# Cumulative log decays of a gated DeltaNet block: one transpose, a trip through DRAM and row broadcasts in place of products with ones

## The chip, the cores and the metric

The kernel runs on one core of one Trainium2 chip, in one launch. The metric is the device time in microseconds (us) of that core, the median of several runs. Below, PE is TensorE (matmuls), PEld its weight loads, DVE is VectorE, ACT is ScalarE, POOL is GpSimd, SP is SyncE, whose queue issues most of the loads.

## What is computed

One layer of a hybrid encoder over 1024 tokens of width 1024, in float32: an RMSNorm, one input projection, a gated DeltaNet group (4 heads of 128) and a latent attention group (8 heads) side by side, an output projection, then a squared-ReLU MLP. The part that matters here is the decay of the DeltaNet group. The reference works in chunks of 64 tokens; the kernel does the same mathematics in blocks of 128.

```python
beta = sigmoid(b_logit)
log_a = -exp(a_log) * softplus(a_logit + dt_bias)      # (tokens, heads)
g = cumsum(log_a, axis=-1)                             # inside each chunk
gdiff = g[..., :, None] - g[..., None, :]
decay_strict = exp(where(strict, gdiff, -inf))
decay_causal = exp(where(causal, gdiff, -inf))
a_mat = einsum("bhnid,bhnjd->bhnij", k_beta, k) * decay_strict
t_inv = triangular_solve(eye + a_mat, eye)
p = einsum("bhnid,bhnjd->bhnij", q, k) * decay_causal
q_dec = q * exp(g)[..., None]
```

So for every head two things are wanted from the cumulative sums g: a 128x128 matrix of exp(g_i - g_j) for each of 8 blocks, and the row exp(g) repeated on all partitions, to scale the transposed queries.

## The kernel before, in words

**Stages.** Up to 74 us the input is normalised and transposed and the narrow columns of the projection are made. From about 74 to 297 us lies the stage that the change touches: PE projects q, k and v (`project`, L582 on, the matmuls at L207 to L209, three for each product), with the latent queries and keys beside them, and the DeltaNet heads get ready. From 297 to 345 us the scan over the blocks runs, then attention, the output projection and the MLP follow.

**Who sets the order.** The tasks of the second stage are Python generators, and a small planner (`Weave`, L44) runs them: each `yield step(pe, dve, act, pool, lat)` adds planned costs to the planner's clock, `signal(name, delay)` sets the planned time of an event, and `yield "name"` or `need(tag, n)` waits for an event or for n free tiles of the pools "a" (12 tiles) and "b" (9 tiles of 128x1024 f32). The order in which they come out is the program's order; the framework's scheduler then places the instructions in the queues of the engines, each of which works its queue off in order. A wait at the head of a queue holds up what stands behind it.

**The weights.** Each 512 KB weight tile is loaded by SP (L183, buffers of 3), rounded by ACT to a high part `whi` (L198), and DVE makes the low part `wlo` (L199). The products of a projection need both.

**Decays.** `decays` (L410 on) makes the log decays `loga` [128 tokens, head, block] and, with two small products (L441, L442) into one PSUM bank `ps_gc`, their cumulative sums in columns, `gcol`, as well as `eg`, `egl` and `cdec`. Its event "decays" lets the first head start.

**head_k(h)** (L641 on) needs the same sums as rows on all partitions. POOL fills `rg` with the triangle `upper` times the head's log decays (L647), PE multiplies that with a matrix of ones (L659, two calls of 512 columns), so that each partition of `ps_g` holds the row of cumulative sums. ACT takes the exponential of one partition (L660, `erow`), and eight DVE instructions (L663) subtract `gcol` and apply the mask `neg` to give E; ACT sends the row to DRAM (L667, `d_er`) and takes the exponential of E (L668). Later in `head_k` the keys are transposed (L620, L622), their squares are summed (L682), small operations of a reciprocal square root follow (L155 to L167), and A is products of keys times E (L698, L702), sent to DRAM (L705, `d_A`).

**head_q(h)** reads the keys (L714) and the row exp(g), repeated on all partitions (L715, `er` from `d_er`), multiplies PT by E (L725) and the queries by `er` on POOL (L731), and sends PT and that product out (L726, L732).

**What follows.** `substitute` reads pieces of all four A (L759, `N`) and solves the 32x32 blocks on DVE in 31 steps (L769, L775). `levels` combines them with products on PE (L817), and the scan starts when all levels are done.

Of the kernel before, what the change touches and what calls it, by code (L numbers as in the profile page):

```python
# [11 lines left out]
AF = mybir.ActivationFunctionType  # L12
# [5 lines left out]
P = 128  # L18
# [78 lines left out]
def need(tag, n):  # L97
    return "need", tag, n


def step(pe=0.0, dve=0.0, act=0.0, pool=0.0, lat=0.4):
    return pe, dve, act, pool, lat


def build(tc, a, out):
# [24 lines left out]
    def psum(name, tag="ps"):  # L130
        return pp[0].tile([P, HALF], F32, name=name, tag=tag, bufs=pp[1][tag])
# [83 lines left out]
    def scratch(name, *shape):  # L215
        return dp.tile(list(shape), F32, name=name)
# [4 lines left out]
    d_v = scratch("d_v", P, NT, MH, 64)  # L221
    d_q = scratch("d_q", MH * 64, T)
    d_r = scratch("d_r", MH * ROPE, T)
    d_er = [scratch(f"d_er{h}", T) for h in range(GH)]
    d_kT = scratch("d_kT", GH, P, T)
    d_qd = scratch("d_qd", GH, P, T)
    d_PT = scratch("d_PT", GH, P, T)
# [27 lines left out]
    def btile(name, dt=F32):  # L255
        W.live["b"] += 1
        return lbp.tile([P, T], dt, name=name, tag="b", bufs=NB)

    def free(tag, n=1):
        W.live[tag] -= n  # L260

    def half_tile(name):
        return lp.tile([P, HALF], F32, name=name, tag="hf", bufs=3)
# [16 lines left out]
    def blocks3(t):  # L280
        return t.rearrange("p (b i) -> p b i", i=P)
# [128 lines left out]
    def decays():  # L410
        spt = btile("spt")
        xx, ax, ee, zz, z2, sp = (spt[:, i * 32 : (i + 1) * 32].rearrange("p (h t) -> p h t", h=GH) for i in range(6))
        nc.vector.tensor_tensor(xx, aL, cols[:, C_DT : C_DT + GH].unsqueeze(2).to_broadcast(shp), op=ALU.add)
        nc.vector.scalar_tensor_tensor(ax, xx, -1.0, xx, op0=ALU.mult, op1=ALU.max)
        e1 = nc.scalar.activation(ee, ax, AF.Exp, scale=-1.0).ins
        e2 = nc.scalar.activation(ealog, cols[:, C_ALOG : C_ALOG + GH], AF.Exp).ins
        after(e2, e1, "tables in turn")
        nc.scalar.activation(beta, bL, AF.Exp, scale=-1.0)

        nc.vector.tensor_scalar(zz, ee, 2.0, None, op0=ALU.add)  # L420
        nc.vector.reciprocal(zz, zz)
        nc.vector.tensor_mul(zz, zz, ee)
        nc.vector.tensor_mul(z2, zz, zz)
        nc.vector.tensor_scalar(sp, z2, 1.0 / 19.0, 1.0 / 17.0, op0=ALU.mult, op1=ALU.add)
        for n in (15, 13, 11, 9, 7, 5, 3, 1):
            nc.vector.tensor_mul(sp, sp, z2)
            nc.vector.tensor_scalar(sp, sp, 1.0 / n, None, op0=ALU.add)
        nc.vector.scalar_tensor_tensor(sp, sp, 2.0, zz, op0=ALU.mult, op1=ALU.mult)
        nc.vector.scalar_tensor_tensor(sp, xx, 0.0, sp, op0=ALU.max, op1=ALU.add)
        nc.vector.scalar_tensor_tensor(  # L430
            loga, sp, -1.0, ealog.unsqueeze(2).to_broadcast(shp), op0=ALU.mult, op1=ALU.mult
        )
        nc.vector.tensor_scalar(beta, beta, 1.0, None, op0=ALU.add)
        nc.vector.reciprocal(beta, beta)
        free("b")
        W.signal("decays", 7.0)
        yield step(0.0, 4.0, 2.0, lat=7.0)

        ps = psum("ps_gc")
        la = loga.rearrange("p h t -> p (h t)")  # L440
        mm(ps[:, 0:32], upper, la, start=True, stop=True)  # L441
        mm(ps[:, 32:64], ones, la, start=True, stop=True)  # L442
        g, gl = (ps[:, i : i + 32].rearrange("p (h t) -> p h t", h=GH) for i in (0, 32))
        nc.vector.tensor_copy(gcol, g)
        nc.scalar.activation(egl, gl, AF.Exp)
        nc.vector.tensor_sub(cdec, gl, gcol)
        nc.scalar.activation(eg, gcol, AF.Exp)
        nc.scalar.activation(cdec, cdec, AF.Exp)
        nc.vector.tensor_scalar(eg, eg, -1.0, None, op0=ALU.mult)
        yield step(0.2, 0.5, 0.8)  # L450


    NF = ROPE // 2
# [187 lines left out]
    def head_k(h):  # L641

        yield f"k{h - 1}" if h else "decays"
        yield need("a", 2)
        yield need("b", 2)
        rg = btile(f"rg{h}")
        nc.gpsimd.tensor_tensor(  # L647
            blocks3(rg),
            upper.unsqueeze(1).to_broadcast([P, NT, P]),
            loga[:, h, :].unsqueeze(2).to_broadcast([P, NT, P]),  # L650
            op=ALU.mult,
        )
        Es[h] = E = atile(f"E{h}")
        erow = btile(f"erow{h}")
        yield step(pool=2.3)
        for half in range(2):
            s = slice(half * HALF, (half + 1) * HALF)
            ps = psum("ps_g")
            mm(ps, ones, rg[:, s], start=True, stop=True)  # L659
            nc.scalar.activation(erow[0:1, s], ps[0:1, :], AF.Exp)  # L660
            for b in range(4):
                bb = 4 * half + b
                nc.vector.scalar_tensor_tensor(  # L663
                    E[:, bb * P : (bb + 1) * P], ps[:, b * P : (b + 1) * P], gcol[:, h, bb : bb + 1], neg,
                    op0=ALU.subtract, op1=ALU.min,
                )
        nc.scalar.dma_start(d_er[h].unsqueeze(0), erow[0:1, :])  # L667
        nc.scalar.activation(E, E, AF.Exp)  # L668
        free("b", 2)
        yield step(1.7, 2.1, 2.2)  # L670

        yield f"k{h}"
        _, kT = ys.pop(("k", h))
        nc.scalar.dma_start(d_kT[h], kT)
        ktok[h] = atile(f"ktok{h}")
        token_major(kT, ktok[h])
        kj = lp.tile([P, P], F32, name=f"kj{h}", tag="kj")
        for b in range(NT):  # L680
            s = slice(b * P, (b + 1) * P)
            nc.vector.scalar_tensor_tensor(  # L682
                kj, ktok[h][:, s], 1.0, ktok[h][:, s], op0=ALU.mult, op1=ALU.mult, accum_out=ssk[:, h, b : b + 1]
            )
        nc.vector.tensor_scalar(ssk[:, h, :], ssk[:, h, :], EPS, None, op0=ALU.add)
        nc.vector.reciprocal(ck[:, h, :], ssk[:, h, :])
        nc.vector.tensor_mul(ck[:, h, :], ck[:, h, :], beta[:, h, :])
        nc.vector.tensor_mul(cdec[:, h, :], cdec[:, h, :], ck[:, h, :])
        r = rsqrt(ssk[:, h, :], [NT], "nkr")
        nc.vector.tensor_mul(nk[:, h, :], r, ssk[:, h, :])  # L690
        yield step(0.9, 2.8, 1.2)
        yield need("b", 1)
        A = btile(f"A{h}")
        for b4 in range(2):
            ps = psum("ps_kk")
            for j in range(4):
                s = slice((4 * b4 + j) * P, (4 * b4 + j + 1) * P)
                mm(ps[:, j * P : (j + 1) * P], kT[:, s], kT[:, s], start=True, stop=True)  # L698
            for j in range(4):
                b = 4 * b4 + j  # L700
                s = slice(b * P, (b + 1) * P)
                nc.vector.scalar_tensor_tensor(  # L702
                    A[:, s], ps[:, j * P : (j + 1) * P], ck[:, h, b : b + 1], E[:, s], op0=ALU.mult, op1=ALU.mult
                )
        nc.scalar.dma_start(d_A[h], A)  # L705
        free("b", 2)
        W.signal(f"A{h}", 3.0)
        yield step(1.7, 2.1)

    def head_q(h):  # L710
        yield f"q{h - 1}" if h else "k3"
        yield need("b", 3)
        kT, er, PT = (btile(f"{n}{h}") for n in ("kTq", "er", "PT"))
        nc.sync.dma_start(kT, d_kT[h])  # L714
        nc.sync.dma_start(er, d_er[h].partition_broadcast(P))  # L715
        yield f"q{h}"
        sq, qT = ys.pop(("q", h))
        nc.scalar.activation(sq, qT, AF.Square)
        for b4 in range(2):
            ps = psum("ps_kq")  # L720
            hs = slice(4 * b4 * P, 4 * (b4 + 1) * P)
            for j in range(4):
                s = slice((4 * b4 + j) * P, (4 * b4 + j + 1) * P)
                mm(ps[:, j * P : (j + 1) * P], kT[:, s], qT[:, s], start=True, stop=True)
            nc.vector.tensor_tensor(PT[:, hs], ps, Es[h][:, hs], op=ALU.mult)  # L725
        nc.sync.dma_start(d_PT[h], PT)  # L726
        psq = psum("ps_q2")
        for b in range(NT):
            mm(psq[:, b : b + 1], sq[:, b * P : (b + 1) * P], ones[:, 0:1], start=True, stop=True)
        nc.vector.tensor_scalar(tq[:, h, :], psq[:, 0:NT], EPS, DK * EPS, op0=ALU.add, op1=ALU.mult)  # L730
        nc.gpsimd.tensor_tensor(er, er, qT, op=ALU.mult)  # L731
        nc.sync.dma_start(d_qd[h], er)  # L732
        Es.pop(h)
        free("b", 5)
        free("a")
        W.signal(f"q done {h}")
        yield step(1.8, 1.3, 1.1, 2.3)
# [989 lines left out]
```

## Time and profile before

| | |
|---|---|
| median of 3 runs | 1267.82 us (1267.79 to 1269.14) |
| the profiled execution, its own time | 1267.6 us |
| its span in the trace | 1265.9 us |
| PE busy | 1220.9 us, 96% of the span, 6228 instructions |
| DVE busy | 898.9 us, 71% |
| ACT busy | 655.2 us, 52% |
| POOL busy | 160.1 us, 13% |
| mean granted TensorE clock | 0.992 |

The span is what the trace covers; 1.7 us of the execution's own time lie outside it. Matmuls overlap in the array, so their durations add up to more than the time they take, and a busy PE is not PE at its peak. All times in the trace are counted from the span's start.

### The profile page before, as it was taken

What the parts mean: (1) busy time and instruction counts of PE and PEld (TensorE: products, weight loads), DVE (VectorE), ACT (ScalarE), POOL (GpSimd) and SP (SyncE); (2) the same over time, 40 slices, a digit from 0 to 9 for tenths busy, and PEclk for the clock granted to TensorE, in tenths of its full rate; (3) what the DMA queues carried; (4) which work ended last, traced back from release to release, by engine and by line L of the source; (5) the groups of instructions that cost most, each with busy time, mean ns of one, the idle gap of its engine ahead of it and who ended that gap; (6) DMA issues with size and microseconds to landing.
All of it is one profiled execution on the core that took longest, in us unless ns stands there. A gap on an engine that the chain in (4) does not pass through costs nothing.

```text
span 1265.9 us, 17687 instructions
## 1 busy us (share of the span) xinstructions
PE 1220.9 (96%) x6228; PEld 1032.8 (82%) x6228; DVE 898.9 (71%) x1779; ACT 655.2 (52%) x1201; POOL 160.1 (13%) x148
## 2 busy tenths in 40 slices
PE   7999999999899999999899999999999999999997
PEld 6978888899778878887677888888888888888885
DVE  7678879545646776695986777767666787875665
ACT  6467744326645786675646444445445433343441
POOL 1011001220044553421000000000000000010120
PEclk9999999999999999999989999999999999999999
DMA  5124634735352511123445455554449984656821
GB/s 235 33 77 147 191 121 167 239 80 172 102 154 83 168 50 30 42 68 133 167 162 162 162 179 208 175 191 184 161 161 401 406 308 154 196 175 220 294 75 66
DMA packets 111218, 205.72 MB, mean 163 GB/s; under 512 B 33557, under 2 KB 51989, under 8 KB 111130
## 3 DMA queue, kind: packets, MB, share of 16 engines
q1 hardware_dynamic: 93696, 171.90, 40.6%
q10 hardware_dynamic: 17434, 32.70, 7.0%
q8 instruction: 49, 0.80, 0.3%
q14 instruction: 39, 0.32, 0.1%
HBM read 143.07 MB, written 61.49 MB: 162 GB/s over the span
## 4 chain that ended last, share of the span: by engine, by line
PE 61%; ACT 4%; DVE 4%; DMA 2%; issue 1%; POOL 0%; ACTq 0%; SPq 0%; DVEq 0%; POOLq 0%
PE ps_dn L208 8%; PE ps_dn L209 8%; PE ps_dn L207 8%; PE ps_up L207 7%; PE ps_up L208 7%; PE ps_up L209 7%; PE ps_PT L1061 2%; PE ps_out L207 2%; PE ps_out L209 2%; PE ps_out L208 2%; PE ps_o L1080 1%; PE ps_sc L207 1%; PE ps_o L1079 1%; PE ps_sc L208 1%; PE ps_sc L209 1%
## 5 line engine op out<-in xcount | busy, mean ns | idle before, releaser
L1589 POOL TENSOR_TENSOR rows<-rows,gpost 128x512 f32<-128x512 f32 x12 | 20.1, 1708 | 612.0 <-ACT junk L1586 612.0
L209 PE MATMUL ps_proj<-hThi,wlo 128*128 128x512 f32 x192 | 75.1, 395 | 1.2 <-DVE wlo L199 1.2
L207 PE MATMUL ps_proj<-hThi,whi 128*128 128x512 f32 x192 | 76.1, 396 | 0.0
L208 PE MATMUL ps_proj<-hTlo,whi 128*128 128x512 f32 x192 | 76.1, 396 | 0.0
L1065 DVE TENSOR_TENSOR PTlo<-ps_PT,PThi 128x512 fp32r<-128x512 f32 (+2 forms) x96 | 52.0, 549 | 20.0 <-ACT PThi L1064 19.3
L1064 ACT CAST PThi<-ps_PT 128x512 fp32r<-128x512 f32 (+2 forms) x96 | 45.4, 480 | 30.0 <-PE ps_PT L1061 28.5
L1521 DVE TENSOR_TENSOR dlo<-draw,dhi 128x1024 fp32r<-128x1024 f32 x35 | 44.7, 1293 | 22.8 <-ACT dhi L1520 22.6
L208 PE MATMUL ps_dn<-dlo,dhi 128*128 128x512 f32 x144 | 56.0, 389 | 0.0
L209 PE MATMUL ps_dn<-dhi,dlo 128*128 128x512 f32 x144 | 56.0, 389 | 0.0
L1520 ACT CAST dhi<-draw 128x1024 fp32r<-128x1024 f32 x35 | 36.2, 1050 | 37.3 <-issue 14.0
L207 PE MATMUL ps_dn<-dhi 128*128 128x512 f32 x144 | 55.1, 389 | 0.0
L1035 ACT ACTIVATE Pt<-ps_sc,nm 128x896 f32<-128x896 f32 (+3 forms) x64 | 48.0, 750 | 10.8 <-DVE nm L1033 5.5
L1336 ACT CAST whi<-raw 128x1024 fp32r<-128x1024 f32 (+1 forms) x29 | 26.1, 907 | 51.5 <-PE ps_up L208 47.9
L1061 PE MATMUL ps_PT<-ident,Pt 128*128 128x128 f32 x288 | 46.5, 275 | 3.2 <-DVE PTlo L1065 1.9
L1033 DVE TENSOR_REDUCE nm<-ps_sc 128x1 f32<-128x896 f32 (+3 forms) x64 | 47.8, 749 | 1.2
L1040 POOL TENSOR_TENSOR Pt<-Pt,rs 128x128 f32<-128x128 f32 (+4 forms) x40 | 34.2, 858 | 87.4 <-DVE rs L1038 63.3
L199 DVE TENSOR_TENSOR wlo<-raw,whi 128x1024 fp32r<-128x1024 f32 (+1 forms) x27 | 32.8, 1218 | 17.4 <-ACT whi L198 14.7
L209 PEld LDWEIGHTS ps_proj<-hThi,wlo 128*128 128x128 f32 x192 | 36.1, 188 | 9.2 <-DVE wlo L199 1.7
L1079 PE MATMUL ps_o<-PThi,V 128*128 128x256 f32 (+1 forms) x160 | 40.6, 276 | 2.9 <-DVE o L1086 1.2
L208 PEld LDWEIGHTS ps_proj<-hTlo,whi 128*128 128x128 f32 x192 | 36.1, 188 | 7.4 <-issue 0.5
L207 PEld LDWEIGHTS ps_proj<-hThi,whi 128*128 128x128 f32 x192 | 36.1, 188 | 7.4 <-issue 0.5
L1061 PEld LDWEIGHTS ps_PT<-ident,Pt 128*128 128x128 f32 x288 | 34.0, 140 | 8.5 <-issue 2.5
(596 smaller groups left out, 3973.7 us busy)
## 6 DMA issues: line engine op xcount, KB each, us to landing
draw<-in_w_down_dram SPq DMA_DIRECT2D x47, 512.0 KB
draw<-d_act SPq DMA_DIRECT2D x41, 512.0 KB
raw<-in_w_up_dram SPq DMA_DIRECT2D x40, 512.0 KB
raw<-in_w_down_dram SPq DMA_DIRECT2D x17, 512.0 KB
raw<-in_w_qkvg_dram SPq DMA_DIRECT2D x16, 512.0 KB
d_act<-c SPq DMA_DIRECT2D x16, 512.0 KB
d_act<-s SPq DMA_DIRECT2D x16, 512.0 KB
raw<-d_act SPq DMA_DIRECT2D x15, 512.0 KB
```

The lines of the kernel that those rows point to most:

```text
L207: mm(ps, lhs[0], rhs[0], start=start, stop=False, **kw)
L208: mm(ps, lhs[0], rhs[1], start=False, stop=False, **kw)
L209: mm(ps, lhs[1], rhs[0], start=False, stop=stop, **kw)
L1033: nc.vector.tensor_reduce(nm, ps[:, :npc, :w], axis=AX.XY, op=ALU.max, negate=True)
L1035: nc.scalar.activation(Pt[:, :n].rearrange("p (i w) -> p i w", i=npc), ps[:, :npc, :w], AF.Exp, bias=nm, scale=1.0, accum_out=sm)
L1040: nc.gpsimd.tensor_tensor(Pt[:, :n], Pt[:, :n], rs.to_broadcast([P, n]), op=ALU.mult)
L1061: transpose(ps[:, j * P : (j + 1) * P], Pt[:, b * P : (b + 1) * P], ident)
L1064: nc.scalar.copy(hi[:, :n, cs], ps3)
L1065: nc.vector.tensor_sub(lo[:, :n, cs], ps3, hi[:, :n, cs].bitcast(F32))
L1079: mm(ps[:, cs], V[h][:, b], hi[:, cs], start=(b == 0), stop=False)
L1520: nc.scalar.copy(hi, raw)
L1521: nc.vector.tensor_tensor(lo, raw, hi.bitcast(F32), op=ALU.subtract)
```

## The change

The cumulative sums `gcol` [128 tokens, 32 columns of head and block] are transposed once on PE into the same PSUM bank. ACT writes the rows and their exponentials into a small tile, and one DMA of ACT's queue stores both in DRAM as `d_gr` [2, head, 1024]. Each `head_k` then loads its row of sums onto all partitions with a broadcast DMA of SP's queue into the tile `rg`, and DVE makes E from `rg` in SBUF. The POOL product, the two products with ones, the exponential of one partition, the DMA of `d_er` and one of two "b" tiles go. `head_q` reads `er` from the second half of `d_gr`. The event "decays" is set later in the task, with a planned delay of 2.5 in place of 7.0, and the planned costs of the steps are changed.

```diff
-    d_er = [scratch(f"d_er{h}", T) for h in range(GH)]
+
+    d_gr = scratch("d_gr", 2, GH, T)
...
         free("b")
-        W.signal("decays", 7.0)
         yield step(0.0, 4.0, 2.0, lat=7.0)
...
         nc.vector.tensor_scalar(eg, eg, -1.0, None, op0=ALU.mult)
-        yield step(0.2, 0.5, 0.8)
+
+        pr = ps[0 : GH * NT, P : 2 * P]
+        transpose(pr, gcol.rearrange("p h t -> p (h t)"), ident)
+        st = half_tile("grow_st")[0 : GH * NT]
+        for n, f in enumerate((AF.Copy, AF.Exp)):
+            nc.scalar.activation(st[:, n * P : (n + 1) * P], pr, f)
+        nc.scalar.dma_start(
+            d_gr.rearrange("n h (t i) -> (h t) n i", i=P), st[:, 0 : 2 * P].rearrange("r (n i) -> r n i", i=P)
+        )
+        W.signal("decays", 2.5)
+        yield step(0.3, 0.5, 1.2)
...
         yield f"k{h - 1}" if h else "decays"
         yield need("a", 2)
-        yield need("b", 2)
+        yield need("b", 1)
         rg = btile(f"rg{h}")
-        nc.gpsimd.tensor_tensor(
-            blocks3(rg),
-            upper.unsqueeze(1).to_broadcast([P, NT, P]),
-            loga[:, h, :].unsqueeze(2).to_broadcast([P, NT, P]),
-            op=ALU.mult,
-        )
+        nc.sync.dma_start(rg, d_gr[0, h].partition_broadcast(P))
         Es[h] = E = atile(f"E{h}")
-        erow = btile(f"erow{h}")
-        yield step(pool=2.3)
-        for half in range(2):
-            s = slice(half * HALF, (half + 1) * HALF)
-            ps = psum("ps_g")
-            mm(ps, ones, rg[:, s], start=True, stop=True)
-            nc.scalar.activation(erow[0:1, s], ps[0:1, :], AF.Exp)
-            for b in range(4):
-                bb = 4 * half + b
-                nc.vector.scalar_tensor_tensor(
-                    E[:, bb * P : (bb + 1) * P], ps[:, b * P : (b + 1) * P], gcol[:, h, bb : bb + 1], neg,
-                    op0=ALU.subtract, op1=ALU.min,
-                )
-        nc.scalar.dma_start(d_er[h].unsqueeze(0), erow[0:1, :])
+        yield step(lat=3.0)
+        for b in range(NT):
+            s = slice(b * P, (b + 1) * P)
+            nc.vector.scalar_tensor_tensor(E[:, s], rg[:, s], gcol[:, h, b : b + 1], neg, op0=ALU.subtract, op1=ALU.min)
         nc.scalar.activation(E, E, AF.Exp)
-        free("b", 2)
-        yield step(1.7, 2.1, 2.2)
+        free("b")
+        yield step(0.0, 2.1, 1.1)
...
-        nc.sync.dma_start(er, d_er[h].partition_broadcast(P))
+        nc.sync.dma_start(er, d_gr[1, h].partition_broadcast(P))
```

## Rows read from the trace of the kernel before

**Rows 1.** Windows: busy us and (instructions) of each engine, PEclk, DMA share, GB/s
```profile
73.77:90.00 16.23, 15.00 (x78) 11.91 (x77) 9.63 (x14) 9.23 (x15) 3.80 (x2) 1.00 0.24 75
90.00:162.00 72.00, 72.00 (x384) 59.64 (x383) 61.77 (x234) 50.77 (x70) 4.09 (x3) 1.00 0.48 156
162.00:174.66 12.66, 12.66 (x74) 11.04 (x73) 6.31 (x7) 3.80 (x6) 2.15 (x1) 1.00 0.80 259
174.66:223.50 48.84, 48.84 (x241) 41.18 (x240) 47.30 (x89) 19.94 (x27) 6.03 (x3) 1.00 0.37 130
223.50:241.92 18.42, 18.42 (x98) 15.79 (x98) 8.83 (x11) 6.00 (x9) 1.91 (x2) 1.00 0.84 265
241.92:297.50 55.58, 54.12 (x424) 51.67 (x423) 29.60 (x40) 17.99 (x29) 14.44 (x14) 1.00 0.48 131
```

**Rows 2.** Waits of PE from 75 to 350 us: total, times, longest us
```profile
PE ps_X L817 <- ACT Yl L823: 1.5, 1, 1.5
PE ps_proj L209 <- DVE wlo L199: 1.2, 1, 1.2
```

**Rows 3.** Timeline of PE at 95.9 us: start, us, instruction, count
```profile
95.90 1.02 PE L659 MATMUL ps_g<-rg,ones 128*128 128x512 f32 x2
96.36 0.79 PE L208 MATMUL ps_proj<-hTlo,whi 128*128 128x512 f32 x1
96.99 0.39 PE L209 MATMUL ps_proj<-hThi,wlo 128*128 128x512 f32 x1
97.22 0.39 PE L207 MATMUL ps_proj<-hThi,whi 128*128 128x512 f32 x1
```

**Rows 4.** Single lines: count, ns minimum/median/maximum, first and last start us
```profile
L659 PE MATMUL ps_g<-rg,ones x16: 590/592/595, 82.7 to 145.7; 128*128 128x512 f32 x16
L647 POOL TENSOR_TENSOR rg<-upper,loga x4: 1897/1898/1941, 78.0 to 119.6; 128x1024 f32<-128x1024 f32 x4
L660 ACT ACTIVATE erow<-ps_g x8: 569/584/588, 85.7 to 146.9; 1x512 f32<-1x512 f32 x8
L663 DVE SCALAR_TENSOR_TENSOR E<-ps_g,gcol,neg x32: 332/341/351, 90.2 to 149.6; 128x128 f32<-128x128 f32 x32
L682 DVE SCALAR_TENSOR_TENSOR kj<-ktok x32: 226/291/295, 101.6 to 156.4; 128x128 f32<-128x128 f32 x32
```

**Rows 5.** Timelines of PE, ACT, POOL and DVE near 80 to 89 us
```profile
80.47 1.04 PE L492 MATMUL ps_kr<-ident,rot 128*32 128x128 f32 x8
81.27 0.48 PE L207 MATMUL ps_proj<-hThi,whi 128*128 128x512 f32 x1
82.63 0.22 ACT L448 ACTIVATE cdec<-cdec 128x32 f32<-128x32 f32 x1
83.71 0.58 ACT L603 COPY xr_k<-ps_proj 128x512 f32<-128x512 f32 x1 [0.39 <-ACT krst L494]
84.77 1.90 POOL L647 TENSOR_TENSOR rg<-upper,loga 128x1024 f32<-128x1024 f32 x1 [4.87 <-PE ps_g L659]
84.92 2.83 DVE L608 SCALAR_TENSOR_TENSOR y_k<-xr_k,cols,y_k 128x1023 f32<-128x1023 f32 x1 [2.44 <-ACT y_k L604]
87.67 1.21 DVE L199 TENSOR_TENSOR wlo<-raw,whi 128x1024 fp32r<-128x1024 f32 x1
88.94 0.50 PE L209 MATMUL ps_proj<-hThi,wlo 128*128 128x512 f32 x1 [1.23 <-DVE wlo L199]
89.01 1.27 DVE L608 SCALAR_TENSOR_TENSOR y_k<-xr_k,cols,y_k 128x1022 f32<-128x1022 f32 x1
```

**Rows 6.** The chain that ended last, two waits for loads: start, us
```profile
356.12 5.07 DMA raw<-d_r
417.52 3.58 DMA raw<-in_w_out_dram
```

**Rows 7.** Waits of all engines from 110 to 300 us: total, times, longest us
```profile
ACT whi L198 <- PE ps_proj L208: 9.8, 5, 5.4
```

**Rows 8.** Timeline of ACT's queue: the write of the last head's A
```profile
162.00 0.33 ACTq L705 DMA_DIRECT2D d_A<-A  x1
```

## The prediction

> **What bounds the kernel now.** I read the windows first, cut at the events of the stage that the change touches: the start of the first head's work, the last head's A at 162.00 us [rows 8], the start and the end of the DVE substitution (174.66 and 223.50 us), the first product of the levels (241.92) and the start of the scan (297.50). The reader is to see the PE column: from 90 to 241.92 us PE's busy time equals the window in every row, and in the last window it lacks 1.46 us [rows 1]. The granted clock is 1.00 throughout. Next come PE's waits: between 75 us and the scan two only, one of 1.2 us for a low weight part from DVE and one of 1.5 us in the levels [rows 2] (the others that the view lists are in the scan). So this stage lasts as long as PE's queue is, and every PE instruction taken from it should shorten it, as long as DVE and the loads keep up. DVE is the next engine: 61.77 of 72 us up to the last A, and 47.30 of 48.84 us during the substitution [rows 1]. After the scan starts nothing is changed, and what follows should simply move earlier.
>
> **PE, removed.** Eight calls go, 16 instructions of 592 ns [rows 4]. The durations would add up to 9.5 us, but they overlap. What two of them take is read from starts: from 95.90 to 96.99 us there are two of them and one 512-column matmul of the projection, whose own step is 97.22 - 96.99 = 0.23 us [rows 3]. So two take 1.09 - 0.23 = 0.86, one 0.43, a head 1.72, four heads **6.88 us**.
>
> **PE, added.** One transpose of 128x32 into 32x128. The rotary keys do four of this very shape, eight instructions that hold PE from 80.47 to 81.27 us [rows 5], so one costs 0.20 us. It waits for `gcol`, but the transposes of the rotary keys can stand before it as they do now; without that cover PE would wait some tenths for one DVE copy.
>
> **Head 0.** Its 1.72 us lie just ahead of PE's wait of 1.23 us for `wlo`, which ended at 88.94. If DVE made `wlo` no sooner, the wait would only grow and this head would give nothing. But DVE was late because of POOL: the first convolution instruction began at 84.92 and took 2.83 us where the next of its kind took 1.27, and POOL's product `rg` for head 1 had begun at 84.77 and ran to 86.67 [rows 5]. With that product gone DVE should be 2.83 - 1.27 = 1.56 us earlier and so should `wlo`. Against this, ACT gets two small activations ahead of its copy at 83.71; the nearest row is 0.22 us for 128x32 [rows 5]. With the DMA issue (0.33 for another store [rows 8]) that is between 0, if they stand elsewhere, and 0.8. I take 0.4, as ACT idled 0.39 there. Head 0 gives 1.56 - 0.4 = 1.16 us, with bounds from -0.8 to 1.72; the transpose falls into the wait that is left.
>
> The Trainium skill, page "SBUF — State Buffer", section on the engine ports, says that DVE and GpSimd share a pair of ports as an exclusive lock: a DVE operation with two SBUF inputs and a GpSimd operation that reads SBUF block each other for the whole instruction. By that rule the trace agrees, since 1.56 us of the POOL instruction's remaining 1.75 were added. The rule speaks against the change too: E's operand moves from PSUM to SBUF, so L663 would become such an operation, while POOL's product of the queries (L731) reads SBUF. By it one overlap would cost DVE up to a whole POOL instruction.
>
> In this kernel's rows E is finished before 150 us [rows 4], and POOL has 4.09 us of work from 90 to 162 [rows 1], of which two removed `rg` products are 3.8. So little remains for E to meet, and I take 0 there, at most one such product of about 1.9 us.
>
> **DVE, ACT, POOL.** E keeps its 32 DVE instructions; the nearest with SBUF operands takes 291 ns against 341 [rows 4], 1.6 us less in all. ACT loses eight of 584 ns, 4.7 us, POOL four of 1.9, 7.6 us [rows 4]. None of that is on PE's path beyond head 0; it only widens the margin. The exponential's table must still be fetched for E, so I count no fetch as gone.
>
> **Loads.** Four broadcast loads of 512 KB come in and one store of 32 KB, four of 4 KB go. The nearest loads of 512 KB whose landing is seen took 3.58 and 5.07 us [rows 6]; the store I bound by the same, above, and by 0. The DMA engines are at 0.48 in the window in question [rows 1], and 2 MB at the 259 GB/s of the third window are 8 us of 72 more, so there is room. SP's queue gets four more issues ahead of weight loads. ACT's rounding of weights waits for PE to give back a buffer (9.8 us in five times) [rows 7], not for a load, so the weight loads are early and a short wait of SP costs nothing; its cover is the 10.9 us that one weight tile keeps PE busy (48 products of 0.23). I take 0, bounds 0 and 5.07 once, for the first row, which must also wait for the store.
>
> **At the tail.** The gain must be passed on by the substitution. The last A follows from projected keys and products, which move with PE, and the substitution starts a fixed chain of loads later. But DVE has only 1.54 us to spare in 48.84 there [rows 1], and PE, with less filler left, may meet the levels' waits sooner. Bounds: 0 and everything. The nearest row is the levels' wait of 1.5 us [rows 2]; I take 1.0 as an estimate from it.
>
> **Sum.** Three heads 3 x 1.72 = 5.16, head 0 1.16, tail -1.0: **5.3 us less**. The profiled execution took 1267.6 us (span 1265.9 and 1.7 outside it), 0.2 under the median: 1267.6 - 5.3 = **1262.3 us**. A measurement tells some 0.2%, 2.5 us, from no change, so this is faster.
>
> **Rivals.**
> *Given back before the scan.* The substitution does not start sooner, because the loads of A's pieces or DVE set it, and PE idles in the levels for what it saved: of 6.3 us before the tail 0 to 2 are left, so 1265.6 to 1267.6, 1268 with a little on top. For it: DVE is busy for half of the 12.66 us between the last A and the substitution, waiting for loads at a DMA share of 0.80 [rows 1]. Against: the last A itself lies at the end of 72 us in which PE never paused [rows 1]. Chance 0.18.
>
> *A DVE queue that waits for rows.* E's eight instructions stand in DVE's queue in front of weight splits and convolutions. The planner allows 3.0 us for a broadcast load; the rows say 3.58 to 5.07 [rows 6], and a weight load ahead of it on the same engines may add as much again: 5.07 + 5.07 - 3.0 = 7.1 us a head in the worst case. What passes to PE is less, as split weights lie ready. It decides from (6.3 + 2.5)/4 = 2.2 us that reach PE in each head; with 4 us a head the time is 1267.6 - 6.3 + 16 = 1277. Against it: E of the last head was made by 150 us and its A at 162 [rows 4, 8], so a late row has slack if E stands late in the queue. Chance 0.13.
>
> The Trainium skill, page "DMA: Bandwidth & Descriptors", section "Anatomy of one DMA", gives a fixed cost of about 2.0 us plus bytes over 436 GB/s for one DMA; by it a row lands after an estimated 3.2 us, 0.2 over the plan, and this rival would have no force at all; no row here shows a load of 512 KB landing so fast.
>
> *More than forecast.* Head 0 and the tail give all: 6.88 - 0.2 = 6.7 us, 1260.9; with a shorter wait for `wlo` besides, 1259.7. Chance 0.22.
>
> *It does not do what it says.* The matmuls are gone from the text, and nothing else makes them; I give 0.01 to a time within 0.2% for this.
>
> **How the numbers follow.** Forecast 0.46 (1261.4 to 1264.5), more than forecast 0.22, given back 0.18, DVE's wait 0.13, no effect 0.01. Faster 0.68, same 0.19, slower 0.13. The range runs from 1259.5, just under the best case, to 1268.5, just over the end of the case in which all is given back; left out are the slower case and a little of the first, under 2 in 10.
>
> **What would show it.** Right: no PE instruction named `ps_g`, PE's waits before the scan still under 4 us, the convolution instruction near 85 us at 1.3 us, the last A near 156, the substitution's start near 169 and the scan's start near 292. Given back: a scan at 297 with new waits of PE in the levels. DVE's wait: E from `rg` with idle time ended by the load of `rg`, and PE waiting for `wlo` behind it. Wrong altogether would be a time over 1265.1, or a gain that lies after the scan's start.

## The result, and the profile after

The changed kernel takes **1262.53 us** (median of 6 runs, 1261.33 to 1263.02) against 1267.79 for the kernel before (6 runs, 1264.82 to 1269.14): ratio 0.9948, 95% interval 0.9928 to 0.9968. That is 5.3 us less, where 1262.3 us was forecast. The profiled execution took 1261.33 us (span 1259.6), 6.3 less than the profiled one of before.

First the windows of the kernel after, cut at the same events as [rows 1]: the last head's A now at 157.3 us, the substitution from 171.8 to 219.1, the first product of the levels at 238.0, the scan at 293.9.

```profile
73.77:90.00 16.23, 15.37 (x80) 12.45 (x79) 9.73 (x16) 9.99 (x16) 0.00 (x0) 1.00 0.28 97
90.00:157.30 67.30, 67.30 (x378) 58.26 (x377) 58.15 (x227) 45.49 (x62) 1.29 (x1) 1.00 0.65 193
157.30:171.80 14.50, 14.50 (x82) 12.57 (x81) 6.21 (x12) 5.56 (x9) 1.12 (x1) 1.00 0.86 227
171.80:219.10 47.30, 46.28 (x229) 38.81 (x228) 45.68 (x85) 19.69 (x26) 5.97 (x3) 1.00 0.37 131
219.10:238.00 18.90, 17.85 (x95) 14.76 (x93) 8.87 (x14) 6.00 (x9) 1.91 (x2) 1.00 0.86 265
238.00:293.90 55.90, 54.44 (x424) 51.71 (x424) 29.96 (x40) 18.01 (x29) 14.46 (x14) 1.00 0.50 132
```

PE still fills the second and third window without a gap, and the second is 4.7 us shorter. But PE now pauses for 1.02 and 1.05 us in the fourth and the fifth, where it lacked nothing before. The waits of PE from 75 to 300 us say for what (total, times, longest):

```profile
PE ps_X L812 <- ACT Yl L818: 1.5, 1, 1.5
PE ps_tm L630 <- ACT y_v L621: 1.0, 1, 1.0
PE ps_proj L207 <- ACT whi L198: 0.8, 1, 0.8
PE ps_v L207 <- ACT kvst L574: 0.7, 1, 0.7
PE ps_s L881 <- DVE vtok L635: 0.7, 1, 0.7
PE ps_Y L812 <- DMA El<-d_A: 0.3, 1, 0.3
```

The wait of 1.2 us for `wlo` [rows 2] is gone; a wait of 0.8 us for `whi` near it, three of 0.7 to 1.0 us further on and one of 0.3 are new. All six add up to 5.0 us, where the two of before made 2.7. The timeline of the first head shows the new parts (start, us, engine, line, instruction, count, idle time before it):

```profile
84.57 0.27 PE L452 MATMUL ps_gc<-ident,gcol 128*32 128x128 f32 x1
...
85.62 1.23 DVE L199 TENSOR_TENSOR wlo<-raw,whi 128x1024 fp32r<-128x1024 f32 x1 [1.95 <-ACT whi L198]
...
85.64 0.50 PE L207 MATMUL ps_proj<-hThi,whi 128*128 128x512 f32 x1 [0.80 <-ACT whi L198]
...
86.56 0.41 ACT L455 ACTIVATE grow_st<-ps_gc 32x128 f32<-32x128 f32 x2
...
86.77 3.92 DVE L618 SCALAR_TENSOR_TENSOR y_k<-xr_k,cols,y_k 128x1023 f32<-128x1023 f32 x3
...
86.90 0.50 PE L209 MATMUL ps_proj<-hThi,wlo 128*128 128x512 f32 x1
...
86.99 0.34 ACTq L456 DMA_DIRECT2D d_gr<-grow_st  x1
...
91.03 0.80 SPq L657 DMA_DIRECT2D rg<-d_gr  x2
...
95.96 2.19 DVE L662 SCALAR_TENSOR_TENSOR E<-rg,gcol,neg 128x128 f32<-128x128 f32 x8 [3.56 <-DMA rg<-d_gr]
```

The three convolution instructions take 3.92 us together, 1.3 each; the one that POOL had stretched to 2.83 [rows 5] is back to its size. DVE makes `wlo` before them now, where the kernel before made it between them, so PE starts with `wlo` at 86.90, not 88.94. Then comes the price: E's operand is stored at 86.99, its load is issued at 91.03, and DVE stands still for 3.56 us until it has landed, at 95.96. PE was busy all that time.

Where the two profiled executions part is best seen at landmarks. The lead of the kernel after is 4.7 us at the last A, 3.6 at the scan's first product (297.5 and 293.9), 2.2 at the end of attention (585.1 and 582.9), 1.8 at the MLP's first product (629.6 and 627.8), 5.9 at its first steady tile `T3hi` (695.7 and 689.8), and 6.3 at the end. So four microseconds of this pair's difference arise in the first 65 us of the MLP, where the code is the same. Here is that place in the kernel before, a window and the timeline:

```profile
630.00:640.00 10.00, 8.49 (x20) 6.12 (x20) 10.00 (x23) 2.92 (x6) 0.00 (x0) 0.51 0.20 79
```

```profile
622.56 0.83 SPq L183 DMA_DIRECT2D raw<-in_w_up_dram  x2
...
627.44 1.04 ACT L1336 CAST first_hi<-raw 128x1024 fp32r<-128x1024 f32 x1 [1.64 <-DMA raw<-in_w_up_dram]
...
629.60 0.50 PE L207 MATMUL ps_up<-B11hi,whi 128*128 128x512 f32 x1 [2.58 <-ACT B11hi L1284]
...
630.89 0.79 PE L208 MATMUL ps_up<-B11lo,whi 128*128 128x512 f32 x1 [0.78 <-DVE B11lo L1285]
...
631.48 0.63 PE L209 MATMUL ps_up<-B11hi,wlo 128*128 128x512 f32 x1
```

And in the kernel after:

```profile
630.00:640.00 10.00, 9.27 (x49) 7.36 (x47) 10.00 (x20) 3.53 (x7) 0.00 (x0) 1.00 0.27 107
```

```profile
621.86 0.83 SPq L183 DMA_DIRECT2D raw<-in_w_up_dram  x2
...
625.60 1.05 ACT L1331 CAST first_hi<-raw 128x1024 fp32r<-128x1024 f32 x1 [0.50 <-DMA raw<-in_w_up_dram]
...
627.76 0.49 PE L207 MATMUL ps_up<-B11hi,whi 128*128 128x512 f32 x1 [1.44 <-ACT B11hi L1279]
...
629.10 0.50 PE L208 MATMUL ps_up<-B11lo,whi 128*128 128x512 f32 x1 [0.84 <-DVE B11lo L1280]
...
629.43 0.40 PE L209 MATMUL ps_up<-B11hi,wlo 128*128 128x512 f32 x1
```

Read the last row of each: the same matmul takes 0.63 us in the one and 0.40 in the other. Before, the weights landed later, ACT's cast `first_hi` waited 1.64 us for them, PE stood idle for 2.58 and 0.78 us behind it, and the granted clock then went down to its lower level of 1.2 GHz for nearly the whole window (0.51 of full speed, where the lower level all the way would be 0.50). After, the waits were 0.50, 1.44 and 0.84 us and the clock stayed at 2.4 GHz (1.00). The prediction had said that a gain after the scan's start would make it wrong, so both parts had to be tested.

### The profile page after: what moved, and what is told of

Same layout as the page of the kernel before. It is cut to its first block, busy times and chain, and to the rows that moved or that the text cites. A ratio compares the mean times of both kernels' runs of the same rounds, so it can differ in the third digit from the quotient of the medians.

```text
span 1259.6 us, 17639 instructions
## 1 busy us (share of the span) xinstructions
PE 1212.2 (96%) x6213; PEld 1027.8 (82%) x6213; DVE 894.4 (71%) x1779; ACT 652.3 (52%) x1196; POOL 152.5 (12%) x144
## 4 chain that ended last, share of the span: by engine, by line
PE 64%; DVE 4%; ACT 2%; DMA 1%; issue 1%; POOL 0%; DVEq 0%; ACTq 0%; SPq 0%; POOLq 0%
PE ps_dn L207 8%; PE ps_dn L208 8%; PE ps_dn L209 8%; PE ps_up L208 8%; PE ps_up L209 8%; PE ps_up L207 8%; PE ps_PT L1056 2%; PE ps_out L207 2%; PE ps_out L209 2%; PE ps_out L208 2%; PE ps_o L1075 1%; PE ps_sc L207 1%; PE ps_o L1074 1%; PE ps_sc L208 1%; PE ps_sc L209 1%
## 5 line engine op out<-in xcount | busy, mean ns | idle before, releaser
L1345 ACT ACTIVATE c<-c 128x512 f32<-128x512 f32 (+1 forms) x32 | 26.7, 840 | 28.1 <-DVE c L1457 20.1
```

## The experiments

**The two kernels again, and the products alone.** The first and the second run repeat the two kernels. The third puts PE's products back into the changed kernel, with no other work of them:

```diff
+        for half in range(2):
+            ps = psum("ps_g")
+            mm(blocks3(ps), ones, upper.unsqueeze(1).to_broadcast([P, 4, P]), start=True, stop=True)
         nc.scalar.activation(E, E, AF.Exp)
```

The fourth leaves the kernel before as it is, but makes its products in one pass in place of two (`rg` and `ones` as F32R, with which E is less exact):

```diff
+    ones_r = lp.tile([P, P], F32R, name="ones_r")
+    nc.vector.tensor_copy(ones_r, ones)
...
-        rg = btile(f"rg{h}")
+        rg = btile(f"rg{h}", F32R)
...
-            mm(ps, ones, rg[:, s], start=True, stop=True)
+            mm(ps, ones_r, rg[:, s], start=True, stop=True)
```

> The kernel before once more, for a second trace of it. In the first trace the granted clock fell to the lower level from about 631 to 642 us, after PE had idled at 626 to 631, and the stage from 590 to 650 us lost some 4 us by that, which the kernel after did not lose. If the fall belongs to the kernel before, it shows again at the same place, and about 4 of the 5.3 us between the medians are the clock's and not the products'. If it was chance, this trace has the clock at 1.00 there and a span some 4 us shorter than 1265.9.

> The kernel after once more. If its clock at the entry of the MLP is granted in full as a rule, this trace has 1.00 from 587 to 647 us again, and the scan begins 3 to 4 us sooner than in the kernel before. If that was chance, the clock falls here, and the span is some 4 us longer than 1259.6.

> The kernel after with the eight products with ones put back on PE, of the triangle in place of the log decays, read by nobody. If PE's queue bounds the stage, its scan begins 5 to 7 us later than the kernel after's, near 299 us. If the gain came from POOL, ACT or the smaller need for tiles, it stays within 1.5 us of the kernel after.

> The kernel before with the eight products in the one-pass form (both operands as fp32r, so E is less exact), and all else kept: POOL's product, the exponential of one row, both tiles, no trip through DRAM for the sums. If PE's queue bounds the stage, eight calls of 0.86 us become eight of about 0.23, 5.0 us less, and the scan begins 4 to 5 us sooner than in the kernel before, so the change's whole gain is had without the loads. If the removal of POOL's and ACT's work carried the gain, less than 1.5 us.

Medians, beside 1267.78 for the kernel before (31 runs): before again 1267.62, ratio 1.0 (0.9982 to 1.0019); after again 1261.18, 0.995 (0.9934 to 0.9967); after with products 1264.07, 0.997 (0.9953 to 0.9987); before with one pass 1263.61, 0.9972 (0.9961 to 0.9984). In the two repeats the clock from 630 to 640 us was as before: down in the old kernel (0.70), 1.00 in the new. But the new one's span is 1261.7 us and not 1259.6, since its clock fell elsewhere (0.83 from 220 to 230 us and from 450 to 460). The products alone cost 2.9 us by the medians (the intervals of the kernel after with and without them overlap), and the one-pass form alone gives 4.2. Both are less than expected. By the prediction the eight calls are worth 6.88 us. In one pass a call still takes its step, 0.23 us in place of 0.86, so that 5.0 us were to be had there:

```profile
95.03 0.39 PE L661 MATMUL ps_g<-rg,ones_r 128*128 128x512 f32 x1
95.26 0.39 PE L209 MATMUL ps_proj<-hThi,wlo 128*128 128x512 f32 x1
```

In the kernel with products the lines of PE from 75 to 300 us show them (busy us, mean ns, idle time before):

```profile
L665 PE MATMUL ps_g<-upper,ones 128*128 128x512 f32 x16 | 7.5, 593 | 0.0
```

7.5 us of PE's time is covered by the sixteen, without a wait in front of them. This table holds the first product of the scan, and what lies around it, for all traces (us; one profiled execution of each kernel, with the median of its runs):

| kernel | last A | scan starts | attention ends | first `T3hi` | median |
|---|---|---|---|---|---|
| before | 162.0 | 297.5 | 585.1 | 695.7 | 1267.79 |
| before again | 161.9 | 297.7 | 585.7 | 696.6 | 1267.62 |
| before, warm | 162.1 | 297.7 | 585.3 | 693.3 | 1265.43 |
| before, shifted | 161.6 | 297.2 | 585.3 | 692.5 | 1267.37 |
| after | 157.3 | 293.9 | 582.9 | 689.8 | 1262.53 |
| after again | 156.1 | 293.0 | 586.1 | 691.6 | 1261.18 |
| after, warm | 156.3 | 291.4 | 581.5 | 687.7 | 1260.77 |
| after, shifted | 156.8 | 291.3 | 584.1 | 690.4 | 1261.83 |
| after with products | 161.5 | 296.3 | 585.0 | 690.8 | 1264.07 |
| before, one pass | 157.3 | 294.7 | 584.0 | 691.3 | 1263.61 |
| after with POOL's product | 160.2 | 296.2 | 584.4 | 690.3 | 1262.01 |
| after, later plan | 155.7 | 296.8 | 588.7 | 694.3 | 1261.56 |

The first four rows have the old code in the stage, the next four the new: their scans start at 297.5 and at 292.4 us on the mean. So the stage is worth **5.1 us** by the traces (at the last A it is 4.7 in the profiled pair and 5.3 by the means of the four). With the products put back the last A is late again, at 161.5 against a mean of 156.6, and the scan starts 3.9 us later than the mean, where 5 to 7 was expected. PE's waits from 75 to 300 us are 1.5 us in that kernel and 5.0 in the one after, so a part of the products fills time in which PE would have waited. With the one-pass form in the old code the last A comes 4.6 us sooner than the old mean and the scan 2.8, where 4 to 5 was expected. Here the clock comes in: it fell shortly before the levels in four traces of the lower eight rows, and in none of the first four. The windows are those of the one-pass kernel, the kernel after again, the later plan and the one with POOL's product (the last two follow below):

```profile
220.00:230.00 10.00, 9.94 (x53) 8.28 (x52) 4.85 (x8) 2.70 (x4) 1.90 (x2) 0.83 1.01 327
220.00:230.00 10.00, 9.04 (x36) 7.07 (x36) 3.06 (x5) 2.21 (x3) 1.12 (x2) 0.83 0.98 314
220.00:230.00 10.00, 8.31 (x41) 6.79 (x40) 4.17 (x8) 2.47 (x4) 1.90 (x2) 0.83 0.97 307
230.00:240.00 10.00, 8.16 (x38) 6.98 (x37) 3.75 (x4) 3.94 (x6) 1.06 (x2) 0.84 0.89 284
```

A window of 10 us at 0.83 has lost 1.7 us of full speed, so by that estimate the scan of these four starts some 1.7 us later than their products alone would have it.

One thing the products do not account for: with all of them put back the kernel is still 3.7 us faster than the one before by the medians. 1.2 us of it lie in the stage (the wait for `wlo` is gone, and the scan starts at 296.3 against 297.5). At attention's end that trace leads the old mean by 0.4; behind it, it gains at the MLP's entry, and there the traces of the old code differ among themselves by 4 us (`T3hi` at 692.5 to 696.6). How the remaining 2.5 us divide no run shows.

**Keeping PE busy at the MLP's entry.** Sixteen matmuls of 384 columns go into the idle time in front of the first `ps_up`, in both kernels (their sums are overwritten):

```diff
         ps = psum("ps_up")
+        if p == 0:
+            x0 = moving(B11, 0)[0]
+            for _ in range(16):
+                mm(ps[:, : 3 * P], k_slice(w, 0, 0)[0], x0[:, : 3 * P], start=True, stop=True)
```

> The kernel before with 16 matmuls of 384 columns, whose result is overwritten, in the gap ahead of the first product of the MLP (about 2.7 us, where PE idled 2.6 us before the granted clock fell in both traces of the kernel before). If the fall of the clock follows from that gap and costs about 4 us, the clock stays at 1.00 from 620 to 650 us and the median comes down by 3 to 4 us, to about 1264. If the time in that stage is lost to a late load and not to the clock, the median stays within 1 us of the kernel before.

> The same 16 matmuls in the kernel after, whose gap there is only 1.4 us and whose clock did not fall. They should cost about 1.2 us where the gap is shorter than they are and save the clock in the few executions that lose it: within 1.5 us of the kernel after. The difference between this run and the kernel before with the same filling is then what the changed stage alone gives: 3.5 to 4.7 us by the scan's start in the traces; if it is 5 to 6, the clock had no part in the change's gain.

The next four kernels are measured beside 1267.33 for the kernel before (35 runs). Before, warm: 1265.43, ratio 0.9992 (0.9976 to 1.0008). After, warm: 1260.77, 0.9952 (0.9936 to 0.9967). The window of the warm old kernel that answers to the 0.51 above:

```profile
630.00:640.00 10.00, 8.58 (x41) 6.70 (x40) 9.97 (x23) 4.49 (x10) 0.00 (x0) 1.00 0.15 59
```

With the pause filled the clock stayed up, which agrees with PE's pause as what let it fall; the last section has pauses that say the pause alone does not decide it. The old kernel gains 1.9 us by the medians, where 3 to 4 was expected if the fall cost that much, and its interval still includes no change; the new one has 0.4 less than the run of it above, which was on another chip. The two warm kernels differ by 4.7 us, about what the stage gives alone.

**POOL's product and a later plan.** In the changed kernel, POOL's product is made again into a tile that nobody reads:

```diff
-        yield need("b", 1)
+        yield need("b", 2)
         rg = btile(f"rg{h}")
+        pj = btile(f"pj{h}")
         nc.sync.dma_start(rg, d_gr[0, h].partition_broadcast(P))
+        nc.gpsimd.tensor_tensor(
+            blocks3(pj),
+            upper.unsqueeze(1).to_broadcast([P, NT, P]),
+            loga[:, h, :].unsqueeze(2).to_broadcast([P, NT, P]),
+            op=ALU.mult,
+        )
...
-        free("b")
+        free("b", 2)
```

and in another the planner is told that the broadcast load takes longer:

```diff
-        yield step(lat=3.0)
+        yield step(lat=8.0)
```

> The kernel after with POOL's four products back, written to a tile that nobody reads (and the second tile that it takes). If POOL holds up DVE as in the kernel before, where a convolution instruction beside it took 2.83 in place of 1.27 us, single DVE instructions beside the four products are 1 to 2 us longer again and the scan begins 0.5 to 2 us later. If PE's queue alone counts, the scan's start stays within 0.5 us of the kernel after.

> The kernel after with one planned cost changed: 8.0 in place of 3.0 us for the landing of a row of sums, which is nearer to the 4.0 (store) and 4.9 us (load) of the trace. DVE's wait of 3.56 us for the first row should go. If that wait costs PE something, the scan begins 1 to 2.5 us sooner than in the kernel after; if PE's queue covers it, the scan's start moves by less than 1 us.

With POOL's product: 1262.01, ratio 0.9957 (0.9941 to 0.9973). Its line `wlo` and its waits of PE from 75 to 300 us:

```profile
L199 DVE TENSOR_TENSOR wlo<-raw,whi x27: 951/1224/2842, 56.0 to 549.8; 128x1024 fp32r<-128x1024 f32 x25, 128x768 fp32r<-128x768 f32 x2
```

```profile
PE ps_Y L819 <- DMA El<-d_A: 2.4, 2, 1.8
PE ps_X L819 <- ACT Yl L825: 1.5, 1, 1.5
PE ps_proj L209 <- DVE wlo L199: 1.4, 1, 1.4
```

One `wlo` took 2842 ns in place of 1224, and the wait for `wlo` is back (1.4; 1.2 before). So POOL's product does hold DVE, and the head-0 step of the prediction read that rightly. In this one trace the scan starts 3.8 us later than the mean, where 0.5 to 2 was expected, and some 1.6 us of that are the clock's (0.84 above); the median is only 0.8 over the run of the kernel after above and 0.5 under the first one. By the medians the product is worth less than 1 us at the end; whether one trace's 3.8 us is typical was not tried.

The later plan gave 1261.56, ratio 0.9956 (0.9936 to 0.9975), which is the time without it. DVE's longest wait for `rg` was still 3.2 us, so the number did not take the wait away, and what the wait costs was not tested. The scan's start fits neither expectation: it lies at 296.8, 4.4 us later than the mean, although the last A at 155.7 is the earliest of all. In between PE waited longer (2.3 us for the tile `kvst`, where the kernel after has 0.7) and the clock fell. The profiled execution was the slowest of the ten (1266.64 us), so this is not the kernel as a rule; but it shows that the scan's start in a single trace can be off by 4 us without a change in the median.

**What made the weights late.** In the traces so far one transfer of the queue "q8 instruction" (0.02 MB) fell 1.5 us behind the issue of the first up-projection loads wherever `first_hi` waited 1.4 to 1.6 us (three traces of the old code), and where it waited 0.3 to 0.7 (seven traces) it fell 4 us or more behind the issue or was not seen around it. If that queue carries PE's instructions, then taking PE instructions out has moved the transfer. A few tiny products at the very start, in time in which PE is idle, should move it and leave the rest nearly as it is (8 calls in the kernel before, 10 in the one after):

```diff
+    for _ in range(8):
+        mm(gmix[0][0:16, 0:16], ones[:, 0:16], ones[:, 0:16], start=True, stop=True)
     for n in range(2):
         mm(gmix[n], ones[0:1, :], grow[:, n * HALF : (n + 1) * HALF], start=True, stop=True)
```

> Kernel before with 8 tiny products (16 wide) in PE's idle time at the very start, nothing else; they only push 16 more PE instructions into PE's stream. In three traces of the old code (before, b_again, b_warm) one transfer of the queue 'q8 instruction' falls 1.5 us after the issue of the first up-projection loads, the cast first_hi then waits 1.4 to 1.6 us for that load, and PE's first ps_up waits 2.4 to 2.6; in the seven traces of other code the transfer falls 4 us or more after the issue or ahead of it, and first_hi waits 0.3 to 0.7. Theory (position of the instruction transfer): the transfer moves some 2 us ahead of the issue of the loads, first_hi waits 0.7 or less, ps_up 1.2 to 1.6, and the granted clock stays at 1.00 from 630 to 640 us; scan start unchanged at 297.5 (plus up to 1 us for the start), median 1265 to 1266, 2 us under before. Rival (the delta of load time comes from something else in the old code): first_hi 1.4 to 1.6 again, ps_up 2.5, lower clock, median 1267.5.

> Kernel after with 10 such tiny products (20 PE instructions) at the very start. Theory: the q8 transfer, 8 us behind the issue of the first up-projection loads in after, moves to about 1 to 3 us behind it; first_hi then waits 1.2 us or more (0.50 in after), ps_up 2.0 or more (1.44), the clock falls near 630 to 640 us, and the median rises to about 1263, while the scan still starts near 293.5. Rival: first_hi stays at 0.3 to 0.7 and the median at 1261 to 1262 wherever the transfer falls.

Beside 1267.79 for the kernel before (17 runs): before shifted 1267.37, ratio 0.9991 (0.9978 to 1.0003); after shifted 1261.83, 0.9953 (0.9935 to 0.9971). In the trace of the shifted new kernel, the transfer in the half microsecond from 623.0 us (queue: packets, MB, share of 16 engines), then timeline and window:

```profile
q8 instruction: 1, 0.02, 12.0%
```

```profile
621.55 0.83 SPq L183 DMA_DIRECT2D raw<-in_w_up_dram  x2
...
626.26 1.04 ACT L1333 CAST first_hi<-raw 128x1024 fp32r<-128x1024 f32 x1 [1.47 <-DMA raw<-in_w_up_dram]
...
628.42 0.50 PE L207 MATMUL ps_up<-B11hi,whi 128*128 128x512 f32 x1 [2.41 <-ACT B11hi L1281]
```

```profile
630.00:640.00 10.00, 9.27 (x38) 7.00 (x38) 10.00 (x23) 3.47 (x8) 0.00 (x0) 0.83 0.20 79
```

The transfer moved from 8.0 to 1.5 us behind the issue, and the old picture came with it: 1.47 us for `first_hi`, 2.41 us of idle PE, the lower clock (0.83). In the shifted old kernel it moved ahead of the issue by 1.5 us, `first_hi` waited 1.17 us, PE 2.1, and the clock stayed at 1.00: half of what was expected. So both moves went the way that was expected, and of all twelve traces the four with the transfer 1.5 us behind the issue have the four longest waits of `first_hi` (1.44 to 1.64 us). That the transfer itself delays the loads, and not something else that moves with PE's instructions, is likely but not shown. The price is not what was expected. The shifted new kernel is 0.7 us above the run of it without a shift, not 2, and the shifted old one 0.4 below its neighbour. The MLP's entry gives 4.1 of the profiled pair's 6.3 us; in the medians it is worth 0 to 2 us.

That the clock does not carry the gain as a whole can be read from all the runs, since each has its mean granted clock on record. It is 0.9916 over the 93 runs of the kernel before that were taken with these experiments, and 0.9920 over the 16 of the kernel after. Among the 93, a run is 0.8 us shorter for each 0.001 that its clock is higher. By an estimate from these numbers the clock accounts for 0.3 us of the difference.

## Why the prediction was right

**The time and the bound.** PE's queue set the stage, and PE work taken from it went from the time: forecast 5.3 us, measured 5.3 by the first comparison and 6.6 by the second (1267.78 - 1261.18); the scans' starts show 5.1. The direction and the rough size are the mechanism's. That the first comparison met the forecast to a tenth is luck, as the second shows.

**PE removed** (6.88). Right in place and kind: no `ps_g` is left, and the products alone move the last A by 4.9 us (156.6, the mean of the four, to 161.5). What reaches the time is less than the term: by the medians 2.9 of 6.88 us for the products put back, and 4.2 of 5.0 for the one-pass form. The term was taken whole for three heads, without a deduction for the waits, on ACT above all, that come up behind the products.

**PE added** (0.20). The one transpose took 0.27 us, ahead of a wait, as put.

**Head 0** (1.16). The mechanism held: without POOL's product the convolution is at 1.3 us, and with it `wlo` grows to 2842 ns. ACT's two activations took 0.41 us, the 0.4 that was taken. But the new order makes `wlo` first, and PE's wait turned into one of 0.8 us for `whi`; the term can't be read off alone.

The Trainium skill, page "SBUF — State Buffer", section "SBUF: two separate sides", says that a DVE operation with two SBUF inputs and a GpSimd operation that reads SBUF lock each other out, for the whole instruction. The stretched `wlo` agrees: 1.6 us more, beside POOL products of 1.9. Whether E from SBUF can be held in the same way no run shows. POOL had no instruction from 75 to 156 us, E's last one began at 137.1, and the 32 took 340 to 352 ns each.

**E on DVE** (1.6 us less). This step was wrong. `kj` with 291 ns was taken as the nearest row; E from `rg` took 344 ns, where it took 341 from PSUM [rows 4]:

```profile
L662 DVE SCALAR_TENSOR_TENSOR E<-rg,gcol,neg x32: 340/344/352, 96.0 to 137.1; 128x128 f32<-128x128 f32 x32
```

Eight in a row take 2.19 us, and took 2.16 before. So it made no difference where this operand lay; the nearer row was E itself. It cost the sum nothing, since DVE's time was put at no gain on the path.

**Loads** (0, bounds 0 and 5.07). The store took 4.0 us and the first load 4.9 from issue to DVE's start, inside the bounds; PE did not notice. (48 products of 0.23 us are 11.0 us, not 10.9; nothing hangs on it.)

The Trainium skill, page "DMA: Bandwidth & Descriptors", section "Anatomy of one DMA — SWDGE (gpsimd) path", gave an estimated 3.2 us for that load. The section is about transfers that GpSimd issues, and this one was issued by SP; the trace's 4.9 us decides for it.

**The tail** (-1.0). At the last A the four traces of the new code lead by 5.3 us, 1.0 less than the 6.3 that was put there; at the scan by 5.1, so the tail took 0.2 and not 1.0. By these means the sum came out through two errors against each other: less arrived at the last A, and less was given back behind it. The tail is not sized well, though: in the profiled pair it was 1.1 (4.7 and 3.6), as forecast, and set against the old means the four traces give 1.0, 1.3, -0.5 and -1.1.

**The rivals.** "A DVE queue that waits for rows" happened, once, for 3.56 us, and had no force, as split weights lay ready. "Given back before the scan" did not happen as a rule; the trace of the later plan looks like it. "More than forecast" (6.7 us) can't be told from the forecast: one comparison gave 5.3, the other 6.6. Landmarks named ahead: last A near 156 (156.1 to 157.3), the substitution near 169 (171.8 in the profiled trace, 169.6 again), the scan near 292 (291.3 to 293.9). PE's waits before the scan were to stay under 4 us; they are 4.3 in the profiled trace of the kernel after (its 5.0 less 0.7 inside the scan), and 3.3 in the repeat.

**What the prediction missed** is the claim that what follows the scan simply moves earlier. By the means of four traces each, the lead is 5.1 us at the scan and 1.7 at the end of attention (585.35 and 583.65), and grows again behind it. Two of the four new traces show the lower clock in the later part of attention and none of the old (at 360 to 370 us all have 0.83): in the shifted new kernel

```profile
450.00:460.00 10.00, 9.30 (x58) 8.40 (x56) 8.01 (x23) 6.34 (x16) 2.86 (x4) 0.85 0.00 0
550.00:560.00 10.00, 8.87 (x54) 7.96 (x53) 8.64 (x25) 5.75 (x14) 1.44 (x2) 0.83 0.05 18
```

From 330 to 350 us three of the four new traces also have less than the old: the two windows lose 3.4 to 3.5 us of full speed together, and 1.7 in all the others of the eight. Added up and averaged, the clock takes an estimated 3.0 of the 3.4 us that are given back up to the end of attention. Why the clock falls in these executions and not in others was not settled; with it, one execution's end says little about a change of 5 us, and the medians are needed.

## What to carry to other kernels

Where PE's busy time equals the window over a whole stage, PE instructions taken out of that stage go from the time in good part (here 2.9 of 6.88 us and 4.2 of 5.0, until other engines' waits set the pace), even in exchange for a trip through DRAM of some 9 us, as long as the rows that come back have work of others to hide behind. Compare the two traces at landmarks and not only at the end: here 2.7 of the profiled pair's 6.3 us lay in code that was not touched. Put the lost microseconds there to the test before crediting the change with them, and take the price of an operation from the same operation's row, not from a like one with other operands.

## What was not expected of the hardware

- The place of a transfer of the queue "q8 instruction" shifts with the number of PE instructions ahead of it, here by 6.5 us for twenty in one kernel and 3 us for sixteen in the other, and where it fell 1.5 us behind two loads of 512 KB the cast behind them waited about 1 us longer (1.47 against 0.50).
- After PE waits of 2.4 to 2.6 us and of 0.5 to 0.8 us a moment later, the granted clock went to the 1.2 GHz level in the window from 630 us (0.51, 0.70 and 0.83 in three traces); with waits of 2.1 and 0.8 us in the shifted old kernel, and 1.44 and 0.84 in the one after, it did not. But it fell to 0.83 with waits of 1.2 and 1.0 us in the kernel with products, and to 0.86 with 1.3 and 1.0 in the one with POOL's product, while the later plan had the same 1.3 and 1.0 and kept 1.00. So the length of the pause alone doesn't decide it.
- A DVE subtraction with a mask of 128x128 f32 takes the same time from SBUF (344 ns) as from PSUM (341 ns).
